# Layer 1's heads: early row blocks, the gate multiplied into the normed tile, and GpSimd's queue in written order

## The chip, the core and the metric

The kernel runs on one NeuronCore of a Trainium2 chip. The core has a matrix engine (TensorE, "PE"), with its weight loads shown apart ("PEld"), a vector engine (VectorE, "DVE"), an activation engine (ScalarE, "ACT"), a general engine (GpSimd, "POOL"), a queue engine (SyncE, "SP"), and 16 DMA engines that move data between HBM and the on-chip buffers. A transfer is issued by one of the engines: here SP issues the weights and most loads, GpSimd a few kinds of transfer that are named below. Each engine works through its own instructions in order. An instruction that waits holds up everything behind it on its engine.

The metric is the device time of the whole program in microseconds.

## The reference

A streaming encoder step of two layers, over 512 tokens of a new stream (the prompt) and 8 running streams with 16 new tokens each (the sample), 2048 wide. Each layer is: RMSNorm with shift and scale from a conditioning vector, a mixer, a SiLU gate, an output projection and a gated addition to the stream. Layer 0's mixer is stick-breaking attention, layer 1's is gated linear attention (GLA) of four heads with key width 256 and value width 512. The change is in layer 1:

```python
def gla_chunk(S, inp):
    q, k, v, g = inp
    b = jnp.cumsum(g, axis=1)
    b_last = b[:, -1]
    q_in = q * jnp.exp(b)
    a = jnp.einsum('bchd,bshd->bhcs', q_in, k * jnp.exp(-b))
    a = jnp.where(jnp.tril(jnp.ones((C, C), dtype=bool)), a, 0.0)
    o = jnp.einsum('bhcs,bshe->bche', a, v) + jnp.einsum('bchd,bhde->bche', q_in, S)
    S = jnp.exp(b_last)[..., None] * S + jnp.einsum('bshd,bshe->bhde', k * jnp.exp(b_last[:, None] - b), v)
    return S, o
...
    o = o * lax.rsqrt(jnp.mean(o * o, axis=-1, keepdims=True) + EPS) * g_out.astype(f32).reshape(GLA_HEADS, GLA_DV)
    y = (o.reshape(B, T, nv) * jax.nn.silu(r.astype(f32))).astype(h.dtype) @ w_out
```

For the sample each of the 8 sequences comes with a state `S` of 256 x 512 for each head, which is read (`q_in S`), updated and returned. The kernel holds it in tiles of 128 x 512 (256 KB), of which there are 64 (8 sequences, 4 heads, 2 halves of the keys); each is loaded once and stored once.

## The kernel before, in words

All products run in float32 precision as three passes over a high and a low half: `halves` makes the high half with a cast on ACT and the low one with a subtraction on DVE. A weight is loaded raw (`wraw`), split, and its two halves are called `wh` and `wl`; those of the gated output are `ogh` and `ogl`.

Around the change stands the stage of layer 1's heads, from about 2000 to 2425 us of the span. Two streams of work are woven together there. The first is plain matrix products. `plain` (its matmuls are L651) makes the rest of the q and k projections for heads 1 to 3, and when it ends, `share(g, og1, w_out1)` (L697) makes the output projection of head g out of the gated output's rows. The other stream is in "lanes":

- `decays` makes the decay factors of a head (L1630).
- `prompt_lane` goes through 16 units, one for each head and chunk of 128 tokens: scores, products with the state `S`, norm, and then `leave`: four transposes (L1593) into PSUM, the product with the gate (L1594), and the store of the product to a scratch array `og_d` in HBM. The root for the norm (`on_r`, L234) is a small instruction on GpSimd.
- `sample_lane` goes through four heads with four groups of four state tiles `s0`. For each group PE reads the four states (L1855, into `ps_z`), then makes the update's product (L1861), and DVE adds it to the state (L1863). The state is then stored (`leaves`), and 7 us later the next load is asked for (`ask`). Seven buffers hold the states.
- `fetches` loads the rows of `og_d` again, 16 of them, and splits them for the output projection. It begins with a head's rows once both lanes are through with that head.

What sets the order: PE's instructions stand in the order in which the program writes them. A small planner, the class `Side`, does the weaving: it keeps a modelled PE time `pe["now"]`, and `drive` lets each lane continue between the blocks of the plain products when the lane's own pause has passed (`step`). Besides, `after(wait, what)` puts a piece of work on a list that is due at a modelled time. All pauses ("7 us later" above) are in this modelled time. The orders of the other engines are made by a scheduler out of what the program writes. `move` (L78) puts a transfer on GpSimd's queue: loads and stores of states (`s<-in_state_gla_dram`, `out_dram<-s`), the store of the prompt's final state (`out_dram<-S`), stores of the gated output (`og<-gate`) and loads of gate tiles (`gate<-gr`).

The words "group 2.4" mean head 2, fourth group, with heads counted from 0 and groups from 1.

Of the kernel before, what the change touches and what calls it, by code (L numbers as in the profile page):

```python
# [15 lines left out]
P = 128  # L16
# [25 lines left out]
def hybrid_step_kernel(ctx: ExitStack, tc: tile.TileContext, A: dict, O: list):  # L42
# [234 lines left out]
    class Side:  # L277
# [10 lines left out]
        def after(self, wait, what):  # L288

            self.due.append((pe["now"] + wait, what))  # L290

        def share(self, **bufs):
            self.free = {k: [0.0] * n for k, n in bufs.items()}
# [386 lines left out]

    y_t = {}

    def share(g, og, w, leave=None, at=None, first=None):


        src = w.rearrange("(kt p) n -> p kt n", p=P)
# [23 lines left out]
        def made():  # L710
            return [t.rearrange("p (a n) -> p a n", a=2) for t in split(raws.pop(0))]

        w0, w1 = made(), made()
        for c in range(4):
            ws = [w0, w1]
            if c < 3:
# [776 lines left out]
        k0 = 4 * g + 2 * i  # L1493
        return w_out1.rearrange("(kt p) n -> p kt n", p=P)[:, k0:k0 + 2, 512 * c:512 * c + 512]

    with tc.tile_pool(name="gl", bufs=1, reuse_waits="tile") as gl:
        came = {"plain": False, "last": False, "of": 0, "when": 0.0}

        def keep(dst, hh):
            t = []  # L1500

            def leave(nt, pt):
# [11 lines left out]

        others = plain(h2, src, [(n0 + P * hh, keep(dst, hh)) for h in range(1, GH)
                                 for n0, dst in ((256 * h, gq_d[h]), (NK + 256 * h, gk_d[h])) for hh in range(2)],
                       lambda: came.update(plain=True))
        for _ in range(2):
            next(others)

# [68 lines left out]
        def leave(h, t0, on, g):  # L1589

            tp = bank("tp")
            for s in range(4):
                turn_block(tp[:, P * s:P * s + P], block(on[:, P * s:P * s + P]), ident)  # L1593
            dve.tensor_tensor(g, tp.rearrange("p (s t) -> p s t", s=4), g, op=ALU.mult)  # L1594
            move(og_d[h][:, :, t0:t0 + P], g)


        ready, through = {}, {"p": 0, "s": 0}
# [63 lines left out]
        def prompt_lane():  # L1662
# [25 lines left out]
            def leave_left():  # L1688
                nonlocal left
                u, on = left  # L1690
                left = None
                h, c = units[u]
                leave(h, P * c, on, gs.pop(u))
                side.after(5.0, lambda: fetch_gate(u + GP))
                if c == 3:
                    through["p"] = h + 1

# [93 lines left out]
        def sample_lane():  # L1791
# [11 lines left out]
            for h in range(GH):  # L1803
# [43 lines left out]
                for n in range(4):  # L1847
                    dt, e = n // 2, n % 2
                    group = [(h, e, dt, m) for m in range(4)]
                    while any(x not in states for x in group):  # L1850
                        yield step(0.3)
                    yield step(max(since, max(states[x][1] for x in group) + 13.0) - pe["now"], tiled=True)
                    for m in range(4):
                        l = qz[e][:, dt, 32 * m:32 * m + 32]
                        mm(o[32 * m:32 * m + 32, :], l, by(l, states[group[m]][0]), start=False, stop=n == 3,  # L1855
                           skip_group_check=True)
                    for m in range(4):
                        yield step(0.3, tp=1)
                        pt = bank("tp")
                        l = kst[e][:, m, :]  # L1860
                        mm(pt, l, by(l, vst[:, m, :]), start=True, stop=True)  # L1861
                        s0 = states[group[m]][0]
                        dve.scalar_tensor_tensor(s0, s0, es[:, dt, 2 * m + e:2 * m + e + 1], pt,  # L1863
                                                 op0=ALU.mult, op1=ALU.add)
                        side.after(1.0, lambda x=group[m]: leaves(x))
                    if n == 1:
                        yield from stack(1)
                        yield step(1.5)
# [5 lines left out]
                if h + 1 < GH:  # L1874
                    yield step(4.0)
                    here = fetch(h + 1)

        def fetches():

            def free(kt):  # L1880
                g, s = kt // 4, kt % 4
                return came["plain"] and came["shares"] >= min(2, g if s > 1 else g - 1)

            rows = {}

# [1 line left out]
                rows[kt] = gl.tile([P, T], F32, tag="pl", name="og_in", bufs=2)  # L1887
                load(rows[kt], og_d[kt // 4][:, kt % 4, :])

            for kt in range(10):  # L1890
                while min(through.values()) <= kt // 4 or not came["last"]:
                    yield step(0.5)
                if kt not in rows:
                    yield step(5.0)
                    ask_rows(kt)
                    if kt % 4 < 3 and kt < 9 and came["plain"]:
                        ask_rows(kt + 1)
                    yield step(4.0)
                while not free(kt):
                    yield step(0.3)  # L1900
                n = 20 + 2 * kt % 12
                og1[kt] = slot(n, name="ogh"), slot(n + 1, name="ogl")
                halves(*og1[kt], rows.pop(kt))
                if kt % 4 < 3 and kt < 9 and kt + 1 not in rows:
                    ask_rows(kt + 1)
                came["rows"], came["at"] = kt + 1, pe["now"]
# [3 lines left out]
        for x in (decays(), prompt_lane(), sample_lane(), fetches()):  # L1910
            side.add(x)
        drive(others)
        with tc.tile_pool(name="w4", bufs=1, reuse_waits="tile") as w4:
            ring3["pool"] = w4
            first = [wraw(w_of(0, 0, i), 2, 512) for i in range(2)]
            for g in range(2):
                side.until(lambda: came["rows"] >= 4 * g + 4 and pe["now"] > came["at"] + 2.0)
                drive(share(g, og1, w_out1, first=first))
                came["shares"] = g + 1
                first = [wraw(w_of(g + 1, 0, i), 2, 512) for i in range(2)]  # L1920
            ring3["pool"] = None
            parts = [split(r) for r in first]
            first = [wraw(w_of(3, 0, i), 2, 512) for i in range(2)]
            side.finish()


    share_banks(mm=8)
# [96 lines left out]
```

## Time and profile before

| | us |
|---|---|
| median of 3 runs | 2552.77 |
| lowest, highest | 2548.27, 2553.05 |
| the profiled execution | 2548.99 |
| its span | 2547.3 |
| PE busy in it | 2438.0 |
| DVE, ACT, POOL busy | 1581.5, 995.4, 162.4 |

The mean granted clock of that execution was 0.982 of full speed. In a view, a row such as `s<-in_state_gla_dram` names what is written and what is read by the program's names; at a row's end stands in brackets how long the engine had been idle ahead of it and what ended this. Time is in microseconds from the start of the span, and L1855 is line 1855 of the kernel before.

### The profile page before, as it was taken

To read this page: it belongs to the slowest core of one execution; us is meant where nothing else is said; L and a number is where in the kernel's file an instruction comes from. 1 tells how busy PE (TensorE), PEld (TensorE's weight loads), DVE (VectorE), ACT (ScalarE), POOL (GpSimd) and SP (SyncE) were. 2 spreads that over 40 slices of the span, in tenths; PEclk is the share of its full clock that TensorE was granted. 3 is DMA by queue.
4 is the path that set the end of the run, shared out by engine and by line. 5 is a ranking of instruction groups with operands and counts; after the bars stand their busy time and mean duration, and the time that the engine had idled before them with its cause. 6 is when DMAs were issued, how large, how long until landed. Compare 5 with 4: busy or idle time off the path is not lost.

```text
span 2547.3 us, 43980 instructions
## 1 busy us (share of the span) xinstructions
PE 2438.0 (96%) x17561; PEld 2156.7 (85%) x17561; DVE 1581.5 (62%) x2565; ACT 995.4 (39%) x1730; POOL 162.4 (6%) x390
## 2 busy tenths in 40 slices
PE   7899999999999999999999989999999999979998
PEld 5589999999999989788887768999999988857776
DVE  5675655556566656666775677566767465555456
ACT  4332222222223335555452454333333454455223
POOL 0010000000000000000000000000000233243100
PEclk8899999999999999999999989999999999989999
DMA  9966666666663367788864754344444777785634
GB/s 344 330 212 223 208 206 214 229 215 214 202 201 116 120 198 223 249 247 264 258 206 124 233 168 124 95 127 134 117 115 118 211 231 242 231 284 192 211 119 146
DMA packets 469439, 503.13 MB, mean 198 GB/s; under 512 B 42730, under 2 KB 366450, under 8 KB 469106
## 3 DMA queue, kind: packets, MB, share of 16 engines
q1 hardware_dynamic: 446274, 436.60, 54.6%
q0 software_dynamic: 16048, 51.92, 6.1%
q10 hardware_dynamic: 6912, 11.80, 1.2%
q8 instruction: 138, 2.26, 0.4%
q14 instruction: 67, 0.55, 0.1%
HBM read 411.10 MB, written 89.13 MB: 196 GB/s over the span
## 4 chain that ended last, share of the span: by engine, by line
PE 74%; DMA 7%; DVE 5%; ACT 3%; issue 3%; POOL 1%; ACTq 0%; SPq 0%; POOLq 0%; DVEq 0%
PE ps_mm L592 38%; PE ps_mm L697 11%; PE ps_mm L651 6%; PE ps_mm L367 3%; PE ps_tp L1080 2%; DMA gv<-kr 2%; PE ps_tp L1132 1%; PE ps_mm L516 1%; PE ps_tp L1040 1%; PE ps_z L1016 1%; PE ps_z L180 1%; PE ps_tp L1546 1%; PE ps_z L1094 1%; ACT wh L134 1%; PE ps_z L222 1%
## 5 line engine op out<-in xcount | busy, mean ns | idle before, releaser
L592 PE MATMUL ps_mm<-sums,wh 128*128 128x320 f32 x2752 | 615.7, 312 | 3.8 <-ACT wh L134 3.8
L592 PEld LDWEIGHTS ps_mm<-sums,wh 128*128 128x128 f32 x2752 | 459.7, 189 | 12.9 <-issue 7.0
L592 PE MATMUL ps_mm<-h,wh 128*128 128x320 f32 x2064 | 461.8, 312 | 4.8 <-DVE u L598 4.8
L592 PE MATMUL ps_mm<-sums,wl 128*128 128x320 f32 x1376 | 426.7, 310 | 1.4 <-DVE wl L135 1.4
L135 DVE TENSOR_TENSOR wl<-wr,wh 128x1024 fp32r<-128x1024 f32 x194 | 237.3, 1224 | 243.9 <-ACT wh L134 238.2
L592 PEld LDWEIGHTS ps_mm<-h,wh 128*128 128x128 f32 x2064 | 343.1, 188 | 20.8 <-issue 12.1
L134 ACT CAST wh<-wb 128x1024 fp32r<-128x1024 f32 x170 | 178.4, 1050 | 428.1 <-PE ps_mm L592 357.3
L134 ACT CAST wh<-wr 128x1024 fp32r<-128x1024 f32 x194 | 203.7, 1050 | 351.0 <-PE ps_mm L592 185.6
L592 PE MATMUL ps_mm<-h,wl 128*128 128x320 f32 x1032 | 318.8, 309 | 0.0
L651 PE MATMUL ps_mm<-h,wh 128*128 128x320 f32 x1152 | 268.7, 320 | 8.9 <-ACT wh L134 4.4
L592 PEld LDWEIGHTS ps_mm<-sums,wl 128*128 128x128 f32 x1376 | 259.4, 189 | 1.9 <-DVE wl L135 1.9
L135 DVE TENSOR_TENSOR wl<-wb,wh 128x1024 fp32r<-128x1024 f32 x170 | 207.9, 1223 | 63.7 <-ACT wh L134 63.2
L651 PEld LDWEIGHTS ps_mm<-h,wh 128*128 128x128 f32 x1152 | 195.9, 192 | 25.5 <-issue 12.3
L697 PE MATMUL ps_mm<-wh,ogh 128*128 128x512 f32 x460 | 201.4, 438 | 4.7 <-DVE y L702 3.5
L592 PEld LDWEIGHTS ps_mm<-h,wl 128*128 128x128 f32 x1032 | 193.7, 188 | 0.0
L697 PE MATMUL ps_mm<-wh,ogl 128*128 128x512 f32 x460 | 181.2, 394 | 0.3 <-DVE ogl L135 0.3
L697 PE MATMUL ps_mm<-wl,ogh 128*128 128x512 f32 x460 | 181.3, 394 | 0.0
L651 PE MATMUL ps_mm<-h,wl 128*128 128x320 f32 x576 | 180.4, 313 | 0.7 <-DVE wl L135 0.7
L697 PEld LDWEIGHTS ps_mm<-wh,ogh 128*128 128x128 f32 x460 | 87.2, 189 | 33.4 <-issue 18.2
L651 PEld LDWEIGHTS ps_mm<-h,wl 128*128 128x128 f32 x576 | 110.4, 192 | 1.0 <-DVE wl L135 1.0
L697 PEld LDWEIGHTS ps_mm<-wh,ogl 128*128 128x128 f32 x460 | 86.8, 189 | 20.7 <-DVE ogl L135 0.7
L697 PEld LDWEIGHTS ps_mm<-wl,ogh 128*128 128x128 f32 x460 | 87.5, 190 | 11.2 <-issue 0.2
(357 smaller groups left out, 3733.7 us busy)
## 6 DMA issues: line engine op xcount, KB each, us to landing
ar<-in_w_ada_dram SPq DMA_DIRECT2D x160, 512.0 KB
wb<-in_sb_w_in_dram SPq DMA_DIRECT2D x82, 512.0 KB
kc<-in_cache_sb_k_dram SPq DMA_DIRECT2D x64, 512.0 KB
vc<-in_cache_sb_v_dram SPq DMA_DIRECT2D x64, 512.0 KB
wr<-in_gla_w_in_dram SPq DMA_DIRECT2D x51, 512.0 KB
wb<-in_gla_w_in_dram SPq DMA_DIRECT2D x45, 512.0 KB
wr<-in_sb_w_in_dram SPq DMA_DIRECT2D x44, 512.0 KB
ar<-in_w_ada_dram SPq DMA_DIRECT2D x64, 256.0 KB
```

Source lines behind the costliest of these rows:

```text
L134: nc.scalar.copy(hi, x)
L135: (e or dve).tensor_tensor(lo, x, hi.bitcast(F32), op=ALU.subtract)
L180: mm(acc[32 * q:32 * q + 32, :w], cT[:, kt + m, :], by(cT[:, kt + m, :], rs[m // each][:, m % each, q, :]), start=kt + m == 0, stop=kt + m ...
L222: mm(acc[32 * j:32 * j + 32, :256], cT[:, kt + m, :], by(cT[:, kt + m, :], r[:, 256 * j:256 * j + 256]), start=kt + m == 0, stop=kt + m == ...
L367: mm(acc[a], l[:, c], by(l[:, c], r[:, k2, :]), start=kt == k0 and first, stop=kt == k0 + nk - 1 and last)
L516: mm(acc[a], l, by(l, r[:, e, :]), start=j == 0 and e == 0 and begun, stop=j == 7 and e == 1 and last)
L592: mm(acc, l[:, k, :], by(l[:, k, :], r), start=start and k == 0 and first, stop=k == 7 and last, skip_group_check=True)
L651: mm(acc[nt], l[:, k, :], by(l[:, k, :], r), start=k0 == 8 and k == 0 and first, stop=k0 == 0 and k == 7 and last)
L697: mm(acc, l, by(l, r[:, e, :]), start=i == 0 and e == 0 and first, stop=i == 1 and e == 1 and last)
L1016: mm(z[:, :n], q[:, hh, qs], by(q[:, hh, qs], k[:, hh, :n]), start=True, stop=True)
L1040: mm(o[:, :P], l, by(l, aT[:, kb, :]), start=kb == 0, stop=kb == qb)
L1080: turn_block(tp[:, P * c:P * c + P], block(kc[:, c, P * hh:P * hh + P]), ident)
```

## The change

The change does six things, all in the stage of layer 1's heads.

1. `after` keeps its list sorted by due time.
2. GpSimd's queue (`manual_schedule`) stands through the stage in the order in which the program writes it, no more in one that the scheduler makes.
3. A state is stored 2.0 us after its update in modelled time (before: 1.0), and the next load is asked for 7.0 us after that, as before. A gate tile's load is asked for 3.0 us after the unit has left (before: 5.0).
4. `leave` writes the gated product into the normed tile `on` instead of the gate's tile, and the store of it is asked for 2.5 us later.
5. The pool `w4`, which holds the output projection's weights, is open from the stage's start. `fetches` loads rows 0 to 2 of head 0's gated output into two of its tiles while the plain products still run. `upper`, called when the last product but one ends, asks for the first two weights of `share(0, ...)` and splits the first; the rows 0 to 2 are split then. The other rows come as before.
6. `share` can stop between the splits of its first two weights (`apart`).

```diff
@@ class Side
         def after(self, wait, what):
 
             self.due.append((pe["now"] + wait, what))
+            self.due.sort(key=lambda x: x[0])
@@ share
-        w0, w1 = made(), made()
+        w0 = made()
+        if apart:
+            yield
+        w1 = made()
@@ the stage
-    with tc.tile_pool(name="gl", bufs=1, reuse_waits="tile") as gl:
+    with tc.tile_pool(name="gl", bufs=1, reuse_waits="tile") as gl, \
+            tc.tile_pool(name="w4", bufs=1, reuse_waits="tile") as w4:
         came = {"plain": False, "last": False, "of": 0, "when": 0.0}
+        queue = ExitStack()
+        queue.enter_context(tc.manual_schedule(engines={mybir.EngineType.Pool}))
...
-                       lambda: came.update(plain=True))
+                       lambda: upper())
@@ leave
-            dve.tensor_tensor(g, tp.rearrange("p (s t) -> p s t", s=4), g, op=ALU.mult)
-            move(og_d[h][:, :, t0:t0 + P], g)
+            on = on.rearrange("p (s t) -> p s t", s=4)
+            dve.tensor_tensor(on, tp.rearrange("p (s t) -> p s t", s=4), g, op=ALU.mult)
+            side.after(2.5, lambda: move(og_d[h][:, :, t0:t0 + P], on))
@@ prompt_lane
-                side.after(5.0, lambda: fetch_gate(u + GP))
+                side.after(3.0, lambda: fetch_gate(u + GP))
@@ sample_lane
-                        side.after(1.0, lambda x=group[m]: leaves(x))
+                        side.after(2.0, lambda x=group[m]: leaves(x))
@@ fetches
+        begun = []
+
+        def upper():
+            came.update(plain=True)
+            begun.append(share(0, og1, w_out1, first=[wraw(w_of(0, 0, i), 2, 512) for i in range(2)], apart=True))
+            next(begun[0])
...
+            while min(through.values()) < 1:
+                yield step(0.5)
+            yield step(8.0)
+            x = [w4.tile([P, 1024], F32, tag=t, name="og_in") for t in ("wh", "wl")]
+            for n in range(2):
+                load(x[n][:, :T], og_d[0][:, n, :])
+            load(x[0][:, T:], og_d[0][:, 2, :1024 - T])
+            load(x[1][:, T:2 * T - 384], og_d[0][:, 2, 1024 - T:])
+            while not came["plain"]:
+                yield step(0.3)
+            for kt in range(2):
+                halves(*row(kt), x[kt][:, :T])
+                yield step(0.8)
+            to = row(2)
+            halves(*[t[:, :1024 - T] for t in to], x[0][:, T:])
+            halves(*[t[:, 1024 - T:] for t in to], x[1][:, T:2 * T - 384])
+            came["rows"], came["at"] = 3, pe["now"]
...
-            for kt in range(10):
+            for kt in range(3, 10):
@@ the stage's end
-        with tc.tile_pool(name="w4", bufs=1, reuse_waits="tile") as w4:
+        for g in range(2):
+            side.until(lambda: came["rows"] >= 4 * g + 4 and pe["now"] > came["at"] + 2.0)
             ring3["pool"] = w4
...
+            drive(share(g, og1, w_out1, first=first) if g else begun[0])
...
+        queue.close()
```

What this moves shows on two engines. The first place is GpSimd's queue ahead of group 0.4's last load (the last row of the next fence, and the last of the one after it). Names with numbers are single tiles: `s0_...` are state tiles, `out_7_dram` is the sample's returned state, `out_6_dram` the prompt's, `og_0_91` head 0's gated output, `gr_1_104` the gates of head 1. Before:

```order
L78 DMA gate_21542<-gr_0_103 128x4x128
L78 DMA out_7_dram<-s0_21344 128x512
L234 TENSOR_TENSOR on_r_21590<-on_ms_21588,mhalf_79 128x1
L78 DMA og_0_91<-gate_21347 512x1x128
L78 DMA out_7_dram<-s0_21397 128x512
L78 DMA s0_21693<-in_state_gla_dram 128x512
```

With the change:

```order
L234 TENSOR_TENSOR on_r_21594<-on_ms_21592,mhalf_79 128x1
L78 DMA out_7_dram<-s0_21376 128x512
L78 DMA out_6_dram<-S_21040 128x2x512
L78 DMA out_7_dram<-s0_21378 128x512
L78 DMA og_0_91<-on_21439 512x1x128
L78 DMA gate_21649<-gr_1_104 128x4x128
L78 DMA out_7_dram<-s0_21380 128x512
L78 DMA out_7_dram<-s0_21504 128x512
L78 DMA s0_21700<-in_state_gla_dram 128x512
```

The last load stood behind two stores of states and one of `og`; now two more stores of states, the store of `S` and a gate's load stand ahead of it.

The second place is the same queue ahead of group 2.4's last load. Before:

```order
L78 DMA out_6_dram<-S_22883 128x2x512
L78 DMA out_7_dram<-s0_23234 128x512
L78 DMA gate_23437<-gr_3_106 128x4x128
L78 DMA out_7_dram<-s0_23299 128x512
L78 DMA out_7_dram<-s0_23301 128x512
L78 DMA out_7_dram<-s0_23385 128x512
L78 DMA og_2_93<-gate_23321 512x1x128
L78 DMA s0_23508<-in_state_gla_dram 128x512
```

With the change:

```order
L78 DMA og_2_93<-on_23250 512x1x128
L78 DMA gate_23444<-gr_3_106 128x4x128
L78 DMA out_7_dram<-s0_23227 128x512
L78 DMA out_7_dram<-s0_23241 128x512
L78 DMA out_7_dram<-s0_23294 128x512
L78 DMA out_7_dram<-s0_23377 128x512
L78 DMA og_2_93<-on_23403 512x1x128
L78 DMA gate_23539<-gr_3_106 128x4x128
L78 DMA s0_23541<-in_state_gla_dram 128x512
```

The group's four stores and the store of `og` stand ahead of the load in both; a gate's load now does too.

The third place is PE at the end of the plain products, at the reads of group 2.4 (the last rows, `ps_z`). Before:

```order
L651 MATMUL ps_mm<-h,wl 128x320
L1861 MATMUL ps_tp<-vst,kst_20583 128x512 x4
L1593 MATMUL ps_tp<-ident,on 128x128 x4
L1630 MATMUL ps_tp<-alr_in,wa_22805 128x320 x2
L697 MATMUL ps_mm<-wh,ogh 128x512
L697 MATMUL ps_mm<-wl,ogh 128x512
L697 MATMUL ps_mm<-wh,ogl 128x512
L1855 MATMUL ps_z<-s_23409,qz_20582 32x512
...
L1855 MATMUL ps_z<-s_23508,qz_20582 32x512
```

With the change (line numbers are 1 to 8 higher there; the rows left out repeat the three of L698, which stand eight times in all):

```order
L652 MATMUL ps_mm<-h,wl 128x320
L1869 MATMUL ps_tp<-vst,kst_20588 128x512 x3
L698 MATMUL ps_mm<-wh,ogh 128x512
L698 MATMUL ps_mm<-wl,ogh 128x512
L698 MATMUL ps_mm<-wh,ogl 128x512
...
L1600 MATMUL ps_tp<-ident,on 128x128 x4
...
L1638 MATMUL ps_tp<-alr_in,wa_22815 128x320
L1863 MATMUL ps_z<-s_23394,qz_20587 32x512
...
L1863 MATMUL ps_z<-s_23541,qz_20587 32x512
```

Ahead of these reads stand 24 matmuls of the output projection where 3 stood.

More of the change, by code (lines that the diff above doesn't have):

```diff
@@ L681, in hybrid_step_kernel, with share @@
     y_t = {}
-    def share(g, og, w, leave=None, at=None, first=None):
+    def share(g, og, w, leave=None, at=None, first=None, apart=False):
         src = w.rearrange("(kt p) n -> p kt n", p=P)
@@ L1876, in sample_lane, with row @@
                     here = fetch(h + 1)
+        begun = []
[3 more added lines that the diff above has]
+            next(begun[0])
+        def row(kt):
+            n = 20 + 2 * kt % 12
+            og1[kt] = slot(n, name="ogh"), slot(n + 1, name="ogl")
+            return og1[kt]
         def fetches():
@@ L1881, in free @@
                 g, s = kt // 4, kt % 4
-                return came["plain"] and came["shares"] >= min(2, g if s > 1 else g - 1)
+                return came["shares"] >= min(2, g if s > 1 else g - 1)
+            while min(through.values()) < 1:
[15 more added lines that the diff above has]
+            came["rows"], came["at"] = 3, pe["now"]
             rows = {}
@@ L1888, in ask_rows @@
                 load(rows[kt], og_d[kt // 4][:, kt % 4, :])
-            for kt in range(10):
+            for kt in range(3, 10):
                 while min(through.values()) <= kt // 4 or not came["last"]:
-                    yield step(0.5)
+                    yield step(0.3)
                 if kt not in rows:
-                    yield step(5.0)
+                    if kt > 3:
+                        yield step(5.0)
                     ask_rows(kt)
-                    if kt % 4 < 3 and kt < 9 and came["plain"]:
+                    if 3 < kt < 9 and kt % 4 < 3:
                         ask_rows(kt + 1)
@@ L1900, in fetches @@
                     yield step(0.3)
-                n = 20 + 2 * kt % 12
-                og1[kt] = slot(n, name="ogh"), slot(n + 1, name="ogl")
-                halves(*og1[kt], rows.pop(kt))
+                halves(*row(kt), rows.pop(kt))
                 if kt % 4 < 3 and kt < 9 and kt + 1 not in rows:
@@ L1912, in hybrid_step_kernel @@
         drive(others)
-        with tc.tile_pool(name="w4", bufs=1, reuse_waits="tile") as w4:
+        for g in range(2):
+            side.until(lambda: came["rows"] >= 4 * g + 4 and pe["now"] > came["at"] + 2.0)
             ring3["pool"] = w4
[L1915 to L1924, printed above, removed]
+            drive(share(g, og1, w_out1, first=first) if g else begun[0])
+            came["shares"] = g + 1
+            first = [wraw(w_of(g + 1, 0, i), 2, 512) for i in range(2)]
+        ring3["pool"] = None
+        parts = [split(r) for r in first]
+        first = [wraw(w_of(3, 0, i), 2, 512) for i in range(2)]
+        side.finish()
+        queue.close()
     share_banks(mm=8)
```

## The prediction

> **What bounds the kernel now.** I read the page's busy shares first, then what PE waits for in the changed stage, then the windows around those waits, the chain of waits, and last GpSimd's own rows.
>
> ```profile
> span 2547.3 us, 43980 instructions
> PE 2438.0 (96%) x17561; PEld 2156.7 (85%) x17561; DVE 1581.5 (62%) x2565; ACT 995.4 (39%) x1730; POOL 162.4 (6%) x390
> ```
>
> PE is busy for 96% of the span, so PE's matmuls set the end, and the change removes none of them. What it can move is PE's idle time in layer 1's heads. The waits of PE between 1990 and 2425 us (in total, times, longest):
>
> ```profile
> PE ps_z L1855 <- DMA s<-in_state_gla_dram: 20.9, 3, 14.1
> ...
> PE ps_tp L1593 <- DVE S L1749: 0.8, 1, 0.8
> ```
>
> Nearly all of it has one cause: the sample lane's read of a group of four states (L1855) waits for the load of the fourth, which GpSimd issues (`move`, L78). Two of the three waits are long:
>
> ```profile
> 2187.52 1.06 PE L1855 MATMUL ps_z<-s,qz 128*32 128x512 f32 x1 [5.87 <-DMA s<-in_state_gla_dram]
> ...
> 2278.26 1.06 PE L1855 MATMUL ps_z<-s,qz 128*32 128x512 f32 x1 [14.09 <-DMA s<-in_state_gla_dram]
> ```
>
> I call them hole 1 (head 1, group 4) and hole 2 (head 2, group 4). The windows show what they cost besides (columns: length, busy time of PE, weight load, DVE, ACT and Pool with instructions, granted clock, DMA share, GB/s):
>
> ```profile
> 2180.00:2190.00 10.00, 4.13 (x15) 1.37 (x14) 3.35 (x6) 3.16 (x6) 4.03 (x7) 0.70 0.82 258
> 2270.00:2280.00 10.00, 1.74 (x2) 0.18 (x2) 4.24 (x9) 3.12 (x5) 3.66 (x6) 0.50 0.97 359
> 2280.00:2290.00 10.00, 10.00 (x39) 8.07 (x39) 5.24 (x9) 5.10 (x10) 5.39 (x11) 0.85 0.69 221
> 2040.00:2380.00 340.00, 315.57 (x1796) 264.25 (x1796) 200.85 (x350) 175.54 (x329) 117.91 (x200) 0.97 0.74 237
> ```
>
> After hole 2 the granted clock is 0.85 over ten microseconds, so 0.15 x 10 = 1.5 us of work is lost on top of the wait. In the stage PE is idle for 340 - 315.6 = 24.4 us in all. That is the most that any order of transfers could win, some 3 us of clock beside it.
>
> Why the load is late stands in the chain and in Pool's rows around hole 2:
>
> ```profile
> 2191.56 0.87 PE ps_mm L651 x6
> ...
> 2274.14 4.07 DMA s<-in_state_gla_dram
> ...
> 2285.38 2.77 PE ps_mm L697 x12
> ```
>
> ```profile
> 2262.23 0.74 POOL L78 DMA_DIRECT2D out_dram<-S  x1 [3.63 <-DVE s L1863]
> ...
> 2271.62 0.72 POOL L78 DMA_DIRECT2D og<-gate  x1 [3.01 <-issue]
> 2274.14 0.56 POOL L78 DMA_DIRECT2D s<-in_state_gla_dram  x1 [1.80 <-issue]
> ...
> 2278.52 0.76 POOL L78 DMA_DIRECT2D gate<-gr  x1 [0.84 <-issue]
> ```
>
> Hole 2 ends when the load issued at 2274.14 has landed. Between 2262.23 and 2278.52 Pool issues 12 transfers, 11 steps in 16.3 us, so 1.48 us a step, though one issue takes 0.56 us: each next one waits for something that the rows mostly leave unnamed ("issue"). So what ends last is set by how many transfers stand ahead of a group's last load in GpSimd's queue.
>
> **The change, part by part.** PE's order hardly moves. The queue of GpSimd does, and each step of it is priced here by three rows: its issue time (groups of Pool, 2040 to 2380 us) and its landing time (medians of the same stretch, then of the quieter 2290 to 2380).
>
> ```profile
> L78 POOL DMA_DIRECT2D s<-in_state_gla_dram x57 | 31.6, 555 | 50.2 <-DMA out_dram<-s 27.6 <-issue 20.3 <-DMA s<-in_state_gla_dram 1.8
> ...
> L78 POOL DMA_DIRECT2D gate<-gr x17 | 13.2, 775 | 29.9 <-DMA og<-gate 19.6 <-issue 6.7 <-DMA out_dram<-s 3.5
> ```
>
> ```profile
> out_dram<-s POOLq DMA_DIRECT2D x64, 256.0 KB, 4.1
> s<-in_state_gla_dram POOLq DMA_DIRECT2D x57, 256.0 KB, 4.5
> ```
>
> ```profile
> out_dram<-s POOLq DMA_DIRECT2D x18, 256.0 KB, 2.8
> ```
>
> *1. The written order of GpSimd.* Stores are due 2 us (before: 1) after the update of their state, and the loads 7 us after that, but the read of a group still stands in PE's order right behind its last load's request. Before, the scheduler put that load ahead of waiting stores, gate loads and the store of `S`; now it stands behind them. I counted in both orders what stands between the first store of the group before and the group's last load (the store of `S` is of double length and counts as two). The price p of one more transfer ahead of the load lies between 0.56 us (issue time only) and 1.48 us (hole 2's pace). I take 1.0, the middle. The slack that swallows it is PE's arrival at the group's first L1855, less the issue of the last load, less 4.5 us of landing. Pool's issues, and then PE's arrivals, in the same order:
>
> ```profile
> 2058.47 0.55 POOL L78 DMA_DIRECT2D s<-in_state_gla_dram  x1 [0.96 <-DMA out_dram<-s]
> ...
> 2075.97 0.58 POOL L78 DMA_DIRECT2D s<-in_state_gla_dram  x1 [0.73 <-DMA out_dram<-s]
> ...
> 2092.72 0.55 POOL L78 DMA_DIRECT2D s<-in_state_gla_dram  x1 [2.87 <-DMA out_dram<-s]
> ...
> 2145.09 0.54 POOL L78 DMA_DIRECT2D s<-in_state_gla_dram  x1 [1.69 <-DMA out_dram<-s]
> ...
> 2160.20 0.55 POOL L78 DMA_DIRECT2D s<-in_state_gla_dram  x1 [2.53 <-DMA out_dram<-s]
> ...
> 2231.68 0.58 POOL L78 DMA_DIRECT2D s<-in_state_gla_dram  x1
> ...
> 2247.69 0.55 POOL L78 DMA_DIRECT2D s<-in_state_gla_dram  x1 [1.25 <-DMA out_dram<-s]
> ...
> 2328.56 0.55 POOL L78 DMA_DIRECT2D s<-in_state_gla_dram  x1
> ...
> 2357.90 0.54 POOL L78 DMA_DIRECT2D s<-in_state_gla_dram  x1 [0.29 <-DMA out_dram<-s]
> ```
>
> ```profile
> 2062.60 0.64 PE L1855 MATMUL ps_z<-s,qz 128*32 128x512 f32 x4
> ...
> 2080.35 1.06 PE L1855 MATMUL ps_z<-s,qz 128*32 128x512 f32 x7
> ...
> 2096.59 0.62 PE L1855 MATMUL ps_z<-s,qz 128*32 128x512 f32 x1 [0.94 <-DMA s<-in_state_gla_dram]
> ...
> 2151.53 1.05 PE L1855 MATMUL ps_z<-s,qz 128*32 128x512 f32 x6
> ...
> 2168.49 1.06 PE L1855 MATMUL ps_z<-s,qz 128*32 128x512 f32 x8
> ...
> 2238.02 1.06 PE L1855 MATMUL ps_z<-s,qz 128*32 128x512 f32 x8
> ...
> 2255.11 1.07 PE L1855 MATMUL ps_z<-s,qz 128*32 128x512 f32 x8
> ...
> 2334.59 1.07 PE L1855 MATMUL ps_z<-s,qz 128*32 128x512 f32 x8
> ...
> 2362.79 1.06 PE L1855 MATMUL ps_z<-s,qz 128*32 128x512 f32 x8
> ```
>
> So, as head.group, transfers added less slack, at p = 1.0: 0.2: 3 - (-0.4) = 3.4. 0.3: 2 - (-0.1) = 2.1. 0.4: 5 - 0 = 5.0 (PE waits there already, its slack is used up). 1.2: 4 - 1.9 = 2.1. 1.3: 6 - 1.2 = 4.8 (8.29 - 4.5 = 3.8 of slack, less 2.6, since its reads now stand three blocks of L651 earlier, 3 x 0.87). 2.2: 3 - 1.8 = 1.2. 2.3: 4 - 2.9 = 1.1. 3.2: 3 - 1.5 = 1.5. 3.4: 2 - 0.4 = 1.6. In 3.3 PE arrives far behind its loads, and I charge nothing. Sum 22.8 us. With p = 0.56 the same lines give 9.5, with p = 1.48 they give 38.
>
> Behind a waiting L1855 in PE's order stand the plain blocks (L651), and every other engine of the stage is fed by these, so such a wait is paid in full.
>
> *2. Clock.* Three of these waits (0.2, 0.4, 1.3) last over 3 us. I charge each the 1.5 us seen after hole 2: +4.5. The lower bound is nothing. The upper one is 3 x 3.0 = 9, if the 0.70 around hole 1 were all lost work.
>
> *3. Hole 1.* Two transfers are added ahead of its last load, but the store of `S` and the gate that stood there go earlier. I put the wait at 2 us instead of 5.87, and too short for the clock: -3.9 - 1.5 = -5.4. Bounds 0 and -7.4.
>
> *4. Early rows and hole 2.* Rows 0 to 2 of head 0's gated output are loaded while plain blocks still run and split when the last product but one ends, so 24 matmuls of the output projection (before 3) stand ahead of the reads that wait in hole 2. The 21 added ones take 21 x 2.77/12 = 4.9 us, done in time that PE now spends waiting. The load itself does not come sooner: four stores and the store of `og` still stand ahead of it, and now a gate load too. One microsecond more for splits (ACT, DVE) that are out of the stores' way: -6. Bounds: 0, where the load comes later by as much, and -14.09. The four added row loads go on SP's queue, whose loads no wait above names, and three later ones go away; I cost them at nothing. If they held the weights' loads of the plain blocks up, it would be one landing each, some 4 us.
>
> *5. The gated product in a tile of its own.* The multiply (L1594) now writes into `on`, so a gate tile comes free when it has been read, not when the store of `og` has landed. That takes away the 19.6 us that Pool's gate loads waited on `og` stores. PE does not wait for a gate in any row, so it is worth at most the 0.8 us of L1593: -0.8 (bounds 0 and -0.8, by itself).
>
> Sum: 22.8 + 4.5 - 5.4 - 6 - 0.8 = +15.1. The profiled execution took 2548.99 us (1.7 us outside the span), so 2564.1. It stands 3.8 us below the median of the runs (2552.77), so in their terms 2567.9, or **2568 us**.
>
> **The rivals.**
>
> *A, faster: a queue that no longer blocks.* Loads lose 27.6 us behind stores and gates 19.6 us behind `og`. If stores that come later, in an order that matches when their data are ready, no longer hold the queue, then each load is issued when it is asked for, more entries ahead cost nothing, hole 1 shrinks as in item 3 and hole 2 to its half: -5.4 - 7 - 0.8 = -13.2, or 2540. Against it: Pool still has the same number of transfers to issue, and a load behind more stores has to wait for each of them to be taken.
>
> *B, no change: transfers land as fast as in the quiet stretch.* Stores land there in 2.8 us instead of 4.1. With p near 0.56, new waits are 9.5 us with hardly any over 3 us, and the gains -12.2: -2.7, or 2550; with p between that and 1.0 it is 2554. For it: the written order spreads stores. Against it: DMA is busy 0.74 over the whole stretch.
>
> The Trainium skill, "DMA: Bandwidth & Descriptors", section "Anatomy of one DMA - SWDGE (gpsimd) path", gives a transfer from this engine about 2.0 us fixed and its bytes over 436 GB/s. For 256 KB that is an estimate of 2.6 us, as in case B. The trace differs: 4.5 us for these loads, 2.8 only in the quiet stretch.
>
> *C, slower: the forecast itself,* new waits in front of groups 2 to 4 of every head. It decides from p = 0.65 on, where new waits and clock pass the 12.2 us of gains.
>
> *D, early rows do nothing.* If the last load of hole 2 comes later by the time that its added gate and the later stores take, hole 2 stays at 14 and only item 4 falls away: 2574. This is within the range of C.
>
> **How the numbers follow.** A measurement of this kernel can tell about 0.2%, 5 us, from no change, so faster is below 2548 and slower above 2558. C with D 0.57, A 0.29, B 0.14. The likeliest one's own range is 2558 to 2590. The range that I give reaches into A: 2536 to 2588. That leaves out the end of A, and the case in which all of p, clock and holes go to their high ends. Faster 0.29, same 0.14, slower 0.57.
>
> **What would show it.** In the changed kernel's waits of PE, the line of `ps_z` (now L1863) on the states' loads should have some ten waits and 30 to 45 us in total instead of 3 and 20.9: one of some 3 us at about 2066, one of some 5 us at the last group of head 0, one at the third group of head 1. Hole 1 should be near 2 us, hole 2 near 8 and later in the output projection's matmuls. Windows over the new waits should show a granted clock of 0.7 to 0.9. The forecast is wrong if that sum stays under 20 us; it is case A where the Pool groups of loads and gates have also lost their waits on stores and `og`. If the sum is as forecast but the time is not longer, PE's waits were not on the path that I take them for.

## The result, and the profile after

The changed kernel takes 2613.95 us (median of 5 runs, 2610.42 to 2618.12) against 2552.77 us. The ratio is 1.025, with a 95% interval of 1.0235 to 1.0266. The forecast had the sign and missed the size: 15 us were predicted, 61 came.

The first lines of the page of the changed kernel:

```profile
span 2616.4 us, 43996 instructions
PE 2466.3 (94%) x17561; PEld 2167.9 (83%) x17561; DVE 1584.8 (61%) x2566; ACT 996.1 (38%) x1731; POOL 166.9 (6%) x390
```

The span is 69.1 us longer, 8 us more than the medians differ: the profiled execution after is the slowest of its five (2618.12 us), the one before lies 3.8 us under its median. PE makes the same 17561 matmuls and is busy 28.3 us longer with them (2466.3 less 2438.0). The rest is idle time, and the view of PE's waits between 1990 and 2500 us names it:

```profile
PE ps_z L1863 <- DMA s<-in_state_gla_dram: 61.6, 11, 13.5
PE ps_mm L652 <- ACT pl L1513: 4.6, 1, 4.6
```

The reads of a group wait for a load of its states 11 times instead of 3, 61.6 us instead of 20.9: 40.7 us more. With the 28.3 that makes 69.0 of the 69.1. Five of the eleven in PE's timeline:

```profile
2069.55 1.91 PE L1863 MATMUL ps_z<-s,qz 128*32 128x512 f32 x2 [5.34 <-DMA s<-in_state_gla_dram]
...
2113.04 1.92 PE L1863 MATMUL ps_z<-s,qz 128*32 128x512 f32 x2 [6.79 <-DMA s<-in_state_gla_dram]
...
2201.87 1.92 PE L1863 MATMUL ps_z<-s,qz 128*32 128x512 f32 x2 [9.66 <-DMA s<-in_state_gla_dram]
...
2330.98 1.92 PE L1863 MATMUL ps_z<-s,qz 128*32 128x512 f32 x2 [13.54 <-DMA s<-in_state_gla_dram]
...
2432.73 1.92 PE L1863 MATMUL ps_z<-s,qz 128*32 128x512 f32 x2 [6.04 <-DMA s<-in_state_gla_dram]
```

They are groups 0.2, 0.4, 1.3, 2.4 and 3.4. The other six: 1.53 (0.3), 5.25 (1.2), 2.84 (1.4), 3.47 (2.2), 3.21 (2.3) and 3.91 (3.2).

Why the busy time grew with the same work is seen in windows of 10 us that begin where a wait ends (the number ahead of the DMA share is the granted clock):

```profile
2069.50:2079.50 10.00, 9.95 (x41) 7.63 (x42) 4.61 (x6) 2.76 (x4) 1.37 (x4) 0.78 0.53 155
2091.70:2101.70 10.00, 9.97 (x58) 8.69 (x59) 9.12 (x17) 5.51 (x13) 2.92 (x5) 1.00 0.64 196
...
2432.70:2442.70 10.00, 9.97 (x29) 6.73 (x30) 3.70 (x7) 1.38 (x3) 2.79 (x5) 0.68 0.17 68
```

The same windows behind the two long waits of the kernel before:

```profile
2187.50:2197.50 10.00, 9.98 (x50) 8.14 (x51) 5.46 (x11) 5.28 (x9) 4.23 (x8) 0.83 0.62 217
2278.20:2288.20 10.00, 9.94 (x32) 6.76 (x33) 4.44 (x7) 3.79 (x7) 4.35 (x8) 0.76 0.65 207
```

After the wait of 1.53 us the clock stays at 1.00. After each of the ten others (2.84 us and longer) it is between 0.68 and 0.78 over ten microseconds, so 2.2 to 3.2 us of work are lost, some 27 us in the ten windows. The kernel before lost 1.7 and 2.4 us in its two, 4.1, which has to be taken off. To be added are two further windows of the changed kernel: behind a wait of 4.61 us for `pl` (at 2021.1) the clock is 0.75, behind one of 1.99 us at the stage's end (2493.6) it is 0.83, together 4.2 us. So some 27 of the 28.3 us of longer busy time are lost clock; the last microsecond is not accounted for. The Trainium skill, "TensorE: Matmul & The Clock Gate", section "HAM oscillation", says that each wait for a transfer that is longer than an idle window lets the next work start at half clock; the ten windows agree (their reads took 1.91 us instead of 1.05).

And why the loads are late. GpSimd's timeline ahead of the first of these waits:

```profile
2060.98 0.74 POOL L78 DMA_DIRECT2D og<-on  x1 [0.16 <-issue]
2065.71 0.78 POOL L78 DMA_DIRECT2D gate<-gr  x1 [3.99 <-issue]
2066.47 1.64 POOL L78 DMA_DIRECT2D s<-in_state_gla_dram  x3
2069.18 0.54 POOL L78 DMA_DIRECT2D s<-in_state_gla_dram  x1 [1.06 <-issue]
```

The load that PE waits for until 2069.55 is the one issued at 2066.47. Ahead of it the store of `og` is issued, and then the gate's load stands at the head of the queue for 3.99 us while the profile names no cause ("issue"). All four state loads stand behind it, and the fourth waits again. Pool's waits (in total, times, longest) show that this is the rule:

```profile
POOL gate L78 <- issue: 53.6, 15, 5.2
POOL s L78 <- issue: 33.8, 19, 4.4
```

Before the change these rows were:

```profile
POOL s L78 <- issue: 23.7, 17, 3.8
...
POOL gate L78 <- issue: 12.2, 7, 5.5
```

### The profile page after: what moved, and what is told of

Read it like the earlier page. It is cut to its first block, busy times and chain, and to the rows that moved or that the text cites. A ratio compares the mean times of both kernels' runs of the same rounds, so it can differ in the third digit from the quotient of the medians.

```text
span 2616.4 us, 43996 instructions
## 1 busy us (share of the span) xinstructions
PE 2466.3 (94%) x17561; PEld 2167.9 (83%) x17561; DVE 1584.8 (61%) x2566; ACT 996.1 (38%) x1731; POOL 166.9 (6%) x390
## 3 DMA queue, kind: packets, MB, share of 16 engines
q1 hardware_dynamic: 446418, 436.60, 53.1%
## 5 line engine op out<-in xcount | busy, mean ns | idle before, releaser
L593 PEld LDWEIGHTS ps_mm<-sums,wh 128*128 128x128 f32 x2752 | 459.0, 188 | 12.9 <-issue 7.0
L593 PEld LDWEIGHTS ps_mm<-h,wh 128*128 128x128 f32 x2064 | 343.0, 188 | 20.3 <-issue 12.1
L698 PE MATMUL ps_mm<-wh,ogh 128*128 128x512 f32 x460 | 202.5, 440 | 3.9 <-DVE y L703 3.0
L698 PE MATMUL ps_mm<-wh,ogl 128*128 128x512 f32 x460 | 182.4, 396 | 0.3 <-DVE ogl L135 0.3
L698 PE MATMUL ps_mm<-wl,ogh 128*128 128x512 f32 x460 | 182.3, 396 | 0.0
L698 PEld LDWEIGHTS ps_mm<-wh,ogh 128*128 128x128 f32 x460 | 87.8, 191 | 33.8 <-issue 19.5
L698 PEld LDWEIGHTS ps_mm<-wh,ogl 128*128 128x128 f32 x460 | 87.5, 190 | 20.9 <-DVE ogl L135 0.7
L1863 PE MATMUL ps_z<-s,qz 128*32 128x512 f32 x128 | 39.6, 676 | 61.7 <-DMA s<-in_state_gla_dram 61.6
```

Source lines behind the costliest of these rows:

```text
L593: mm(acc, l[:, k, :], by(l[:, k, :], r), start=start and k == 0 and first, stop=k == 7 and last, skip_group_check=True)
L698: mm(acc, l, by(l, r[:, e, :]), start=i == 0 and e == 0 and first, stop=i == 1 and e == 1 and last)
```

## The experiments

Times vary by some us between chips, so each run is compared by its ratio to the kernel before on the same chip.

### Room for descriptors: more, and less

In the trace the gate's load nearly always starts 0.3 to 0.4 us after the `og` store ahead of it has landed (the store issued at 2060.98 lands 4.4 us later, at some 2065.4). An `og` store and a gate load are 512 pieces of 512 bytes each, a state's transfer is 128 pieces of 2 KB. 512 + 3 x 128 = 896 pieces go out in a row, the next 128 wait, and 512 + 512 wait. So a theory R: GpSimd's transfers share a fixed room for descriptors, filled by the number of pieces, and the launch code sets it with `dynamic_dma_scratch_size=1024`. The rival N is the prediction's price: some 1 us for any transfer ahead. Changing that one number leaves every engine's order as it was.

```diff
-    nc = _bacc.Bacc("TRN2", target_bir_lowering=False, num_devices=1, dynamic_dma_scratch_size=1024)
+    nc = _bacc.Bacc("TRN2", target_bir_lowering=False, num_devices=1, dynamic_dma_scratch_size=1728)
```

> The changed kernel with more room for the descriptors of GpSimd's transfers (1728 instead of 1024 bytes of a partition); every engine's order is the same. Theory R (room): in the changed kernel 15 gate loads stood 53.6 us at the queue's head although no data held them, each until the og store ahead had landed, because an og store and a gate load, 512 pieces each, do not fit in the room together, and the states' loads behind a gate stood 33.8 us likewise. With more room these two sums fall below 10 us each, PE's wait for states falls from 61.6 to 15 to 35 us, and the time from 2614 to 2550 to 2580. Theory N (number): what counts is how many transfers stand ahead of a group's last load, each at some 1 us of the DMA engines' time. Then nothing changes: 2605 to 2620, PE's wait 55 to 65 us.

Measured: ratio 1.0166 (1.0134 to 1.0199), median 2590.58. The same place in GpSimd's timeline, and then the waits of PE and of Pool:

```profile
2063.70 0.73 POOL L78 DMA_DIRECT2D og<-on  x1
2064.35 0.78 POOL L78 DMA_DIRECT2D gate<-gr  x1
2065.12 2.17 POOL L78 DMA_DIRECT2D s<-in_state_gla_dram  x4
```

```profile
PE ps_z L1863 <- DMA s<-in_state_gla_dram: 41.6, 9, 11.0
...
POOL s L78 <- issue: 4.0, 10, 1.1
...
POOL gate L78 <- issue: 2.4, 3, 1.9
```

The causeless waits of gates and loads are gone (53.6 to 2.4, 33.8 to 4.0), as R says. PE's waits fall by 20 us, less than R expected, and the time by 0.84%. So room is a cause, and not the only one.

With less room (768 in that line):

> The changed kernel with less room for descriptors (768 bytes of a partition); every engine's order is the same. Theory R: beside a gate load fits one state's transfer instead of three, so loads and stores behind a gate wait for its landing too: the idle time of Pool's rows that names no cause grows by 30 us or more, and the time to 2625 to 2660. Theory N: 2605 to 2620.

Measured: 1.0357 (1.0329 to 1.0385), median 2640.49; PE waits 81.6 us for states. GpSimd behind a gate's load:

```profile
2057.22 0.78 POOL L78 DMA_DIRECT2D gate<-gr  x1 [4.00 <-issue]
2057.98 0.58 POOL L78 DMA_DIRECT2D s<-in_state_gla_dram  x1
2060.64 1.61 POOL L78 DMA_DIRECT2D s<-in_state_gla_dram  x3 [2.08 <-issue]
```

One state's load goes out beside the gate's, where three did: 640 pieces fit and 768 don't. N is out. The three sizes order the time: 2640, 2614, 2591.

### The room is filled by pieces

A third test leaves the room at 1024 and changes the pieces: the gates' scratch array is laid out by chunks of 128 tokens, so that a gate load is 128 pieces of 2 KB, with the same bytes and the same orders.

```diff
-    gr_d = [dp.tile([P, 4, T], F32, name=f"gr_{h}") for h in range(GH)]
+    gr_d = [dp.tile([P, TOK, 4, P], F32, name=f"gr_{h}") for h in range(GH)]
...
-                    store(gr_d[h][:, kt, :], out[s])
+                    store(gr_d[h][:, :, kt, :], out[s].rearrange("p (c t) -> p c t", c=TOK))
...
-            move(g, gr_d[h][:, :, t0:t0 + P])
+            move(g, gr_d[h][:, t0 // P, :, :])
```

> The changed kernel at 1024 bytes, with the gates' scratch array laid out by chunks, so that a gate load is 128 pieces of 2 KB and not 512 of 512 bytes; same bytes, every engine's order the same. Theory R in its full form (what fills the room is the number of pieces): a gate load now fits beside an og store, the gates' idle time without a cause falls from 53.6 to under 12 us; the loads behind still wait for the og store's 512 pieces at times (33.8 to 15 to 30 us). Time from 2614 to 2582 to 2604. If the room is counted in transfers or bytes, nothing changes: 2606 to 2620.

Measured: 1.0138 (1.0108 to 1.0168), median 2583.33. GpSimd's timeline at the same place, then the waits:

```profile
2062.87 0.74 POOL L78 DMA_DIRECT2D og<-on  x1 [0.15 <-issue]
2063.52 0.63 POOL L78 DMA_DIRECT2D gate<-gr  x1
2064.08 0.62 POOL L78 DMA_DIRECT2D s<-in_state_gla_dram  x1
2065.59 0.54 POOL L78 DMA_DIRECT2D s<-in_state_gla_dram  x1 [0.89 <-issue]
```

```profile
PE ps_z L1863 <- DMA s<-in_state_gla_dram: 43.5, 10, 10.4
...
POOL s L78 <- issue: 22.8, 23, 3.3
...
POOL gate L78 <- issue: 6.5, 8, 1.6
```

The gate's load goes out right behind the `og` store (53.6 to 6.5 us). Loads still wait behind the store's 512 pieces. Transfers and bytes are the same as in the changed kernel, so it is pieces that fill the room. The layout alone is worth about what 69% more room is worth (1.0138 and 1.0166, with intervals that overlap).

### The written order

The changed kernel without its second item, so that GpSimd's order is the scheduler's again:

```diff
-        queue.enter_context(tc.manual_schedule(engines={mybir.EngineType.Pool}))
```

> The changed kernel without item 2: GpSimd's order is the scheduler's again, all other items stay. If the written order is the cause of the loss, the time returns to 2535 to 2565 and PE's wait for states to 10 to 30 us. If the loss comes from the other items (early rows on SP's queue, stores and loads that are due later), it stays above 2590.

> The changed kernel without the written order of GpSimd and with more room for descriptors (1728 bytes): the fourth corner of a square with the changed kernel (written, 1024), the run with room alone (written, 1728) and the run without the written order (scheduler, 1024). If order and room cost independently, 2575 - 23 = 2552, PE's wait for states 15 to 25 us, and the 75.8 us of gate loads that name no cause fall below 15. Rival: the room only matters in the written order (in the kernel before it brought nothing): 2568 to 2580.

Measured: with 1024 bytes 1.0109 (1.0073 to 1.0145), median 2575.40, between the two times that had been expected; with 1728 bytes 1.0009 (0.9995 to 1.0023). Waits of the first (PE, Pool) and then of the second (PE):

```profile
PE ps_z L1862 <- DMA s<-in_state_gla_dram: 40.0, 7, 14.3
...
POOL gate L78 <- issue: 75.8, 18, 6.3
```

```profile
PE ps_z L1862 <- DMA s<-in_state_gla_dram: 18.0, 4, 8.2
```

So there is a square of ratios: written order 1.025 and 1.0166 (1024, 1728), scheduler's order 1.0109 and 1.0009. Order costs 0.0141 and 0.0157, some 36 to 40 us; room costs 0.0084 and 0.0100, 21 to 26 us. Within the intervals the two add up, and together they are the whole loss: with both undone, no difference from the kernel before can be told, so what the other items cost or bring cancels out. The scheduler, too, puts the gate's load right behind the `og` store once the tile does not forbid it, and so falls into the same wait (75.8 us).

The kernel before with more room:

> The kernel before with more room (1728 bytes), its orders unchanged. Theory R: there the gate load waits for the og store anyway, since the tile is the same; but 23.7 us of the loads' idle time and 12.2 us of the gates' name no cause and should mostly go. Hole 2 (14.1 us) shortens by 3 to 6 us, hole 1 by 1 to 3: 2538 to 2549. Theory N: no change, 2548 to 2556.

Measured: 1.0000 (0.9986 to 1.0015). PE's wait for states falls from 20.9 to 15.0 us (hole 1 2.73, hole 2 11.85), but the time does not move; R expected 4 us or more. In this kernel the gate has to wait for the `og` store anyway, since both use one tile.

### What in the written order is late

Of the 41.6 us that PE still waits in the run with more room, four waits are 31.9 (the expectation below calls them all fourth groups; the second is 1.3's):

```profile
2112.52 1.91 PE L1863 MATMUL ps_z<-s,qz 128*32 128x512 f32 x2 [8.43 <-DMA s<-in_state_gla_dram]
...
2194.43 1.92 PE L1863 MATMUL ps_z<-s,qz 128*32 128x512 f32 x2 [8.22 <-DMA s<-in_state_gla_dram]
...
2307.42 1.92 PE L1863 MATMUL ps_z<-s,qz 128*32 128x512 f32 x2 [11.04 <-DMA s<-in_state_gla_dram]
...
2405.36 1.81 PE L1863 MATMUL ps_z<-s,qz 128*32 128x512 f32 x2 [4.19 <-DMA s<-in_state_gla_dram]
```

GpSimd's timeline ahead of the first:

```profile
2095.00 0.94 POOL L234 TENSOR_TENSOR on_r<-on_ms,mhalf 128x1 f32<-128x1 f32 x1 [8.56 <-DVE on_ms L232]
...
2099.78 0.72 POOL L78 DMA_DIRECT2D out_dram<-S  x1 [3.29 <-DVE qz L1821]
...
2105.29 1.13 POOL L78 DMA_DIRECT2D s<-in_state_gla_dram  x2
```

The queue stands for data that are late: first the root for the norm, then the store of `S`, 3.29 us, with the load that PE waits for behind them. One run moves the store of `S` alone behind that load, another puts the due times back.

```diff
-                    move(sp_o[0, 0, h].rearrange("(d p) v -> p d v", p=P), S)
+                    side.after(14.0, lambda h=h, S=S: move(sp_o[0, 0, h].rearrange("(d p) v -> p d v", p=P), S))
```

> The changed kernel with more room (1728 bytes) and the store of S due 14 us of modelled time later, which puts it behind the last load of each head's fourth group. With room alone the fourth groups waited 8.4, 8.2, 11.0 and 4.2 us, and the store of S stood 3.3, 3.0, 6.2 us at the queue's head for its data. Theory H: these waits shrink by 3 to 6 us each, in sum from 31.9 to 14 to 22, and the time from 2591 to 2562 to 2580. Theory N (number of transfers ahead, 0.56 to 1.48 us each): the store of S counts as two, so 1 to 3 us each, 2578 to 2588. If neither holds, 2588 to 2594.

Measured: 1.0076 (1.0059 to 1.0093), from 1.0166. The four waits:

```profile
2109.50 1.05 PE L1863 MATMUL ps_z<-s,qz 128*32 128x512 f32 x2 [2.63 <-DMA s<-in_state_gla_dram]
...
2182.24 1.05 PE L1863 MATMUL ps_z<-s,qz 128*32 128x512 f32 x2 [2.01 <-DMA s<-in_state_gla_dram]
...
2288.70 1.91 PE L1863 MATMUL ps_z<-s,qz 128*32 128x512 f32 x2 [7.75 <-DMA s<-in_state_gla_dram]
...
2383.93 1.91 PE L1863 MATMUL ps_z<-s,qz 128*32 128x512 f32 x2 [6.34 <-DMA s<-in_state_gla_dram]
```

In sum 18.7 instead of 31.9 us: the first three shrink by 5.8, 6.2 and 3.3, the last grows by 2.2. The reads of the first two now run at full pace (1.05 us instead of 1.91), and the clock over the ten microseconds behind them is 1.00 and 0.83 instead of 0.69 and 0.69. In time it is some 23 us.

The sums fit theory H, but the trace shows two parts in each of the first two. Measured from PE's arrival at the read, the load is issued 3.5 us earlier at the first place and 2.5 us at the second, near the 3.29 and 2.98 us that the store of `S` had stood at the queue's head for its data. The rest is the landing: 4.9 instead of 7.2 us, and 5.7 instead of 9.4, with that store of 512 KB no longer ahead of the load. By number alone a store of double length could bring 2 x 1.48 = 3.0 us in each, which the first part by itself would not rule out. That the queue stood there for late data is seen in its rows; how much of the gain is this and how much the shorter landing, at the third place too, stays open, and at the last place neither theory holds.

```diff
-                side.after(3.0, lambda: fetch_gate(u + GP))
+                side.after(5.0, lambda: fetch_gate(u + GP))
...
-                        side.after(2.0, lambda x=group[m]: leaves(x))
+                        side.after(1.0, lambda x=group[m]: leaves(x))
```

> The changed kernel (written order) with more room (1728 bytes) and the due times of the kernel before: states stored 1.0 us after the update, gate loads asked 5.0 us after the unit has left. Without the due times' change the run with room alone took 2591. Theory H (head of the queue): what the written order still costs is that transfers whose data are late (the store of S, stores of states, the root for the norm) stand ahead of the last load; 1 us earlier stores make them wait for DVE instead, so little changes: 2580 to 2600. Theory D (due times): the later stores are the rest of the loss, then 2550 to 2572.

Measured: 1.0139 (1.0123 to 1.0155), PE's wait for states 36.7 us. The due times are not the loss.

What of the written order's cost the roots and the state stores make, beside the store of `S`, was not taken apart.

### The reads' place, and a version that is faster

In both kernels of the case the reads stand in PE's order right behind the last load's request, whatever `13.0` in the lane's pause says: the planner runs a tiled step in the same pass that polled for the load. These runs make the pause count, with 4 or 7 us:

```diff
-                    yield step(max(since, max(states[x][1] for x in group) + 13.0) - pe["now"], tiled=True)
+                    yield step(max(since, max(states[x][1] for x in group) + 4.0) - pe["now"])
+                    yield step(0.0, tiled=True)
```

> As the run before it, and the reads of a group stand in PE's order at least 4 us of modelled time behind the last load's request (in both kernels of the case they stand right behind it). Theory P (place of the reads): what is left is only that PE comes too early; PE's wait for states falls under 10 us and the time to 2528 to 2545. Rival: the later reads make the lane longer and every following store and load later, so that the waits come back further on or at the stage's end: 2550 to 2575.

> The kernel before with more room for descriptors and the reads 4 us of modelled time later. Theory P: hole 1 goes, hole 2 shrinks to under 6 us: 2528 to 2542. Rival: hole 2 is not the reads' place but the stores ahead, which wait for DVE: it stays over 10 us and the time within 2543 to 2555.

> The fastest run so far (scheduler's order of GpSimd, 1728 bytes, reads 4 us after the last request: 2542) with the reads 7 us after it. If PE's remaining waits in the stage have nothing to do with the states' loads, 2538 to 2546. If the later reads make the lane too long, 2546 to 2560.

Measured: 0.9977 (0.9961 to 0.9992) for the changed kernel with the scheduler's order, more room and 4 us; 1.0002 (0.9986 to 1.0017) for the kernel before with more room and 4 us; 1.0043 (1.0029 to 1.0057) for the first with 7 us. Two of PE's waits in the first:

```profile
PE ps_tp L1599 <- ACT on L1581: 9.1, 2, 7.7
PE ps_mm L652 <- ACT pl L1512: 5.2, 1, 5.2
```

No wait for states is left in it, nor in the second, and yet they gain 6 us and nothing. In the first PE now waits 7.7 us at 2241 us for the norm's scaling: the lane's later work makes a wait in place of the earlier ones. With 7 us that wait grows to 18.4 us in four places, and one wait for a state, 7.1 us, is back. Why the second gains nothing was not taken apart.

Then the same with the small room, and with gates in 2 KB pieces at both rooms (edits as above):

> The changed kernel without the written order, reads 4 us later, and 1024 bytes as in both kernels of the case (the fastest run had 1728). If the later reads by themselves give the loads time enough, 2538 to 2550. If the gate loads that wait for room (75.8 us in that order) still come through to PE, 2552 to 2572.

> As the run without the written order, with reads 4 us later, at 1024 bytes (2563), and the gate loads in 2 KB pieces. Theory R: its 55.9 us of gate loads that wait for room go, and with them most of what stands between it and the same kernel with 1728 bytes (2542): 2538 to 2552. If the room matters there through the og stores (25.3 us) rather than the gates: 2553 to 2565.

> The fastest run so far (scheduler's order, 1728 bytes, reads 4 us later: 0.9977 of the kernel before) with the gate loads in 2 KB pieces. If 512-byte pieces cost only room, nothing changes: 2537 to 2546. If they also make the transfers themselves slower (gate loads land in a median of 5.7 us there), landings shorten and the time falls to 2530 to 2538.

Measured: 1.0064 (1.0040 to 1.0088), 0.9974 (0.9960 to 0.9987), 0.9986 (0.9974 to 0.9999). Pool's gate loads without a cause in the first and the second:

```profile
POOL gate L78 <- issue: 55.9, 15, 6.6
```

```profile
POOL gate L78 <- issue: 6.8, 4, 2.7
```

At 1024 bytes the pieces decide over 0.9%, 23 us; in the first run the late gates reach PE as waits for the norm's scaling (23.6 us, 10.9 in the second), while states cost it 3.0 us. At 1728 they bring nothing that can be told (0.9977 and 0.9986), so 512-byte pieces cost room, and the last expectation's hope for faster landings fell. The second has the lowest ratio, though the run with more room and reads 4 us later (0.9977) can't be told from it: the changed kernel with GpSimd's order left to the scheduler, reads 4 us later and gates in 2 KB pieces, has a median of 2539.29 us against 2545.83 beside it, 0.26% faster than the kernel before (0.13 to 0.40%).

## Why the prediction was wrong in size

**What bounds the kernel** held: the time went where PE waits for a group's last load, and every place that the sum named is a place of a wait. Summed over the groups of item 1, 0.2 to 3.4 without hole 1 and hole 2, the forecast was 22.8 us and the trace has 44.3 (45.2 less the 0.94 that was there). 0.3, 0.4 and 3.3 came near (1.5 for 2.1, 5.9 for 5.0, none for none); 0.2, 1.2, 1.3, 2.2, 2.3, 3.2 and 3.4 came 1.9 to 4.9 us longer.

**Item 1, the price p, failed.** "The price p of one more transfer ahead of the load lies between 0.56 us (issue time only) and 1.48 us (hole 2's pace)": transfers have no common price. A state's transfer behind free room costs its issue, 0.56 us. At 1024 bytes a gate load behind an `og` store costs the rest of that store's landing, 53.6 us over 15 of them, 3.6 us each, and then holds the loads behind it, 33.8 us over 19. A transfer whose data are late costs the lateness. The upper end, taken from hole 2's pace, was an average over a stretch in which these cases were mixed. The landing, which item 1 took as 4.5 us, was not at fault: the loads that ended the eleven waits landed in 3.0 to 6.5 us, with a median of 4.4.

**Item 5 failed with it.** "That takes away the 19.6 us that Pool's gate loads waited on `og` stores": the tile no longer made the gate wait for the store, and the room did, for more than twice as long. The rows that were quoted had a trace of it: 6.7 us of the gate's idle time and 20.3 us of the loads' were named "issue", with no cause, and the prediction noted that the rows leave the cause unnamed, put it into the pace of 1.48 us, and did not ask what it was. Its -0.8 came: PE has no wait at the transposes of `leave` any more; whether the tile did this no run shows.

**Item 2, the clock, was mis-sized twice.** It charged a long wait at 1.5 us from the window 2280 to 2290. The wait ended at 2278.26, so that window begins 1.7 us too late; from 2278.2 on the granted clock is 0.76, 2.4 us. And ten waits were long enough, not three. With what hole 1 gives back (1.5 in item 3) the sum had 3.0 us of clock; PE's busy time grew by 28.3, of which some 27 are seen as clock.

**Item 3** came near: hole 1 (1.4) is 2.84 us, forecast 2. A window at 0.70 stands behind it, which the forecast ruled out. **Item 4 failed:** hole 2 is 13.54 us and not 8. The 21 matmuls do stand ahead of it, but the last load came later by as much, which is rival D. Of SP's loads only `wa` is named as a new wait of PE in the stage, 0.6 us, so the early rows cost PE next to nothing there, as forecast.

The parts of the miss: waits 40.7 instead of 12.9 (22.8 less 3.9 and 6), which is 27.8; busy time, nearly all of it clock, 28.3 instead of 3.0, which is 25.3. Together 53.1 of the 54.0 us between 15.1 and 69.1.

**The rivals.** A fell: a queue in written order blocks more. Half of its idea is right for another reason, since what blocks is what is late or does not fit. B fell: landings were indeed shorter (the state stores' median is 3.4 us against 4.1), and the time longer. The 2.8 us that the prediction sets beside the loads' 4.5 are the stores' in the quiet stretch; the loads took 3.9 us there (view of DMA issues, 2290 to 2380 us). The Trainium skill, "DMA: Bandwidth & Descriptors", section "Anatomy of one DMA", prices a transfer by bytes and a fixed part; the estimate of 2.6 us from it stays below the median of 3.9 us that the states' loads take in the changed kernel, and neither number decides here, since most of the wait is ahead of the issue.

## What to carry to other kernels

A transfer at the head of GpSimd's queue that waits for nothing the profile names may be waiting for room: look for what landed 0.3 to 0.4 us before it started, and count pieces, not bytes. It need not be: in the run with the scheduler's order, more room and reads 4 us later, a store of `og` waited 9.05 us without a named cause until 2259.70, though the transfer issued last before it had landed by 2255.3; the multiply that fills the store's tile ended only at 2259.1, so it was the data. A scratch array laid out so that a transfer is few long pieces was worth about as much here, at 1024 bytes, as a larger descriptor area; with the larger area it brought nothing that can be told. A written order for a queue should put what others wait for ahead of what is late, and a price for "one more in the queue" should be taken for each kind, beside the clock that a wait of some 3 us and more can cost (here 2.2 to 3.2 us each).

## What the runs showed of the hardware

GpSimd's transfers under way are limited by their descriptors. With 1024 bytes, 896 pieces go out and 1024 don't; with 768, 640 go and 768 don't; with 1728, the 1536 of an `og` store, a gate load and four state loads are under way together (the store issued at 2063.70 lands at some 2068.1, the four loads are issued between 2065.12 and 2067.29). The Trainium skill, "DMA: Bandwidth & Descriptors", section "SWDGE vs HWDGE vs iDMA", says that GpSimd writes a pair of descriptors for each operation into rings in SBUF. That an issue waits while they are full is what these runs add.

The granted clock stayed at 1.00 after a wait of 1.53 us and fell to between 0.68 and 0.78 over the next ten microseconds after every wait of 2.84 us and more for a state in the changed kernel. These runs give no sharp bound: in the run with the later store of `S`, a wait of 2.63 us was followed by reads at full pace (1.05 us), in the run with more room and the old due times one of 3.56 us too (the clock over the ten microseconds behind it was 0.83), and in the changed kernel one of 2.84 us by reads of 1.91 us.
